# Attention heads issued in pairs, and a state-space scan folded by four steps

## The chip, the cores and the metric

The kernel runs on one core of one Trainium2 chip. Its time is the device time of that core in microseconds (us), taken as the median of several executions. A profile of one execution gives each engine's instructions: PE is TensorE (matmuls), PEld its weight loads, DVE VectorE, ACT ScalarE, POOL GpSimd, SP the engine that issues most DMAs.

## The reference, cut to what matters

The program is two transformer-like blocks of two layers over 256 tokens of width 1024. Three attentions and one scan are touched by the change:

```
swa:   s = q k^T * scale, masked to |i-j| <= 128; p = softmax with a sink logit; o = p v   (8 heads on 2 key heads)
diff:  s_c = q_c k_c^T * scale (c = 0, 1); a = softmax(s_0) - lam * softmax(s_1); o = a v  (4 heads)
stick: z = q k^T * scale; w = exp(log_sigmoid(z) + sum of log_sigmoid(-z) over later keys); o = w v  (16 heads)
S5:    x_t = lb * x_(t-1) + bb u_t  (complex, 32 groups of 64 states),  y_t = Re(c x_t) + d u_t
```

The first block has both layers of swa and diff (the mixer); the second block has an S5 layer with a pooling branch, then a stick-breaking layer, each followed by a mixture of 16 experts (MoE).

## The kernel before

All weights stream from memory through a ring of 1 MB tiles. `Ring.pump` issues the next load on SP's queue as soon as a slot is free; the order of loads is fixed. Large matmuls split each f32 operand in a high and a low part and add three products (`S` L381, `T` L390, `proj_T` L435); small ones are plain f32, and each such call shows as two MATMUL instructions. `bank("w")` and `bank("acc")` are two sets of four PSUM banks. The order of the work is written out by hand: every engine runs its instructions in the order in which the program emits them.

**Mixer** (L899). Each step projects one weight unit (some 5.6 us of PE), rotates it, and weaves in one piece of each attention. `swa_scores` (L822) makes the scores of two heads that lie on partitions 0 to 63 and 64 to 127: for each head and each half of the queries one 64-row matmul (L830), then a bf16 mask product over all 128 rows (L833). `diff_scores` (L866, matmul L873) makes first both halves for c = 0, then both for c = 1, again 64 rows each, and without a mask. `swa_soft` and `diff_soft` follow on DVE and ACT.

**S5.** `s5_params` (L1170) makes the tables while the feed-forward layer before runs: it is a generator whose 18 pieces are emitted at the ends of the iterations 2 to 19 of that layer (`hooks`, L2368). The recurrence is folded by two steps, so a scan has 128 columns. POOL builds tables of cosines and sines of 128 columns by doubling (L1232 to L1251); DVE, PE and ACT build the input matrices `BT` (transposes, L1269), the output matrices `CT` and one matrix `K0` (L1304). `s5_layer` (L1345) then has eight rounds of two state blocks each. `inputs(i)` (L1405) is 8 calls over 32 rows with 128 columns; `turned_in(i)` multiplies by the tables (two DVE products, L1414 and L1415, and two POOL sums); `scan(i)` has four scans of 128 columns (L1428), two more products and two POOL sums into `S`. `outputs(h)` (L1435) multiplies `S` by `CT` (L1445, 32 output columns, four next to one another in the array) after `K0` (L1440), once for each half of the state blocks. Between the rounds PE makes the pooling branch (`vproj`, `pooled`, `poolproj`). When `outputs(1)` is emitted, `scanned()` gives the memory of the tables and of `S` to the ring, for the expert weights. Then `trow` (L399) begins the output product.

**Stick-breaking** (`sb_layer`, L2119). `scores` of one head: 64 rows, 256 and 128 columns (L2156, L2157), Abs, Exp, Ln on ACT (L2159 to L2161), one DVE and one POOL operation. `weights`: two bf16 mask products (L2170, L2171), three plain products (L2172 to L2174), Exp on ACT (L2176). `av`: two products into 64 output columns (L2183, L2184). `advance` runs scores of head h, weights of head h-2 and av of head h-4; two steps stand after each of the query and key projections, and the last eight close the stage.

```
            if h < 16:
                step1(h)
            if 2 <= h < 18:
                step2(h - 2)
            if 4 <= h < 20:
                step3(h - 4)
```

Of the kernel before, what the change touches and what calls it, by code (L numbers as in the profile page):

```python
# [8 lines left out]
F32 = mybir.dt.float32  # L9
# [73 lines left out]
class K:  # L83
# [738 lines left out]
    def swa_scores(self, b):  # L822

        nc = self.nc
        outs = []
        for kv in range(2):
            rows = slice(64 * kv, 64 * kv + 64)
            sv = self.bank("acc").rearrange("p (q k) -> p q k", q=2)
            for qt in range(2):
                nc.tensor.matmul(sv[:, qt, :], self.sq[rows, b, qt * P:qt * P + P], self.sk[rows, 0, :],  # L830
                                 start=True, stop=False)
                kb, mk = ((1, self.maskA), (0, self.maskB))[qt]
                nc.tensor.matmul(sv[:, qt, kb * P:kb * P + P], self.ident16, mk, start=False, stop=True)  # L833
            outs.append(sv)
        return outs
# [30 lines left out]
    def diff_scores(self, h):  # L866
        nc = self.nc
        outs = []
        for c in range(2):
            rows = slice(64 * c, 64 * c + 64)  # L870
            sv = self.bank("acc").rearrange("p (q k) -> p q k", q=2)
            for qt in range(2):
                nc.tensor.matmul(sv[:, qt, :], self.dq[rows, h, qt * P:qt * P + P], self.dk[rows, h, :],  # L873
                                 start=True, stop=True)
            outs.append(sv)
        return outs
# [267 lines left out]
    def s5_alloc(self, pool):  # L1144
        t = lambda shape, name: pool.tile(shape, F32, name=name)
        self.tc_, self.ts_ = t([P, 16, P], "s5c"), t([P, 16, P], "s5s")
        self.BT = [[t([P, 4, P], f"BT{c}{b}") for b in range(2)] for c in range(2)]
        self.CT = [t([P, 16, 32], f"CT{i}") for i in range(4)]
        self.K0 = t([P, 4, P], "K0")
        self.prm = t([P, 7, 16], "s5prm")  # L1150
        self.dcol, self.pscale = (self.cp.tile([P, 4], F32, name=n) for n in ("s5d", "pscale"))

# [17 lines left out]
    def s5_params(self, tp):  # L1170
# [7 lines left out]
        for t in BD + [self.K0]:  # L1178
            G.memset(t, 0.0)
# [20 lines left out]
        lbr, lbi, fr, fi, m2, c2, s2 = (self.prm[:, i] for i in range(7))  # L1200
        V.tensor_mul(lbr, mag, cs)
        V.tensor_mul(lbi, mag, sn)
        V.tensor_mul(m2, mag, mag)
        V.tensor_mul(t1, sn, sn)
        V.tensor_scalar(c2, t1, -2.0, 1.0, op0=ALU.mult, op1=ALU.add)
        V.scalar_tensor_tensor(s2, sn, 2.0, cs, op0=ALU.mult, op1=ALU.mult)
# [18 lines left out]
        wc, ws, w2 = sm("wc", [P, 16]), sm("ws", [P, 16]), sm("w2", [P, 16])  # L1225
        G.tensor_copy(wc, c2)
        G.tensor_copy(ws, s2)
        G.memset(self.tc_[:, :, 0:1], 1.0)
        G.memset(self.ts_[:, :, 0:1], 0.0)
        tm = sm("tm", [P, 16, 32])  # L1230
        k = 1
        while k < P:  # L1232
# [13 lines left out]
            if k < P:  # L1246
# [31 lines left out]
        bb = [sm(f"bb{c}", [P, 16, 16]) for c in range(2)]  # L1278
        halves = [(slice(0, 64), lambda t: t[:, :, 0:16]), (slice(64, P), lambda t: t[:, :, 16:32])]
        cmul(bb[0], bb[1], bc16(fr), bc16(fi), b_re, b_im, u, v)  # L1280
        yield
        for c in range(2):
            for rows, o in halves:
                V.tensor_copy(o(BD[c])[rows], bb[c][rows])
        yield
        flat = lambda t: t.rearrange("p n h -> p (n h)")
        for c in range(2):
            transposed(self.BT[c][1].rearrange("p q s -> p (q s)"), flat(BD[c]))
        yield
# [6 lines left out]
        for c, cd in enumerate(cds):  # L1296
            transposed(flat(self.CT[c]), cd.rearrange("p q g s -> p (q g s)"), -1.0 if c else None)
        yield

        pt = self.bank()[:, :P].rearrange("p (q o) -> p q o", q=4)  # L1300
        for n in range(16):
            q, r = divmod(n, 4)
            for c in range(2):
                nc.tensor.matmul(pt[32 * r:32 * r + 32, q, :], BD[c][:, n], self.CT[c][:, n],  # L1304
                                 start=(c == 0), stop=(c == 1))
        yield
        for r in range(4):
            rows = slice(32 * r, 32 * r + 32)
            V.tensor_copy(self.K0[rows, :, rows], pt[rows])
        yield  # L1310
        cmul(BD[0], BD[1], bc16(lbr), bc16(lbi), bb[0], bb[1], u, v, halves)
        yield
        for c in range(2):
            transposed(self.BT[c][0].rearrange("p q s -> p (q s)"), flat(BD[c]))
        yield
        bc32 = lambda a: a[:, :, None].to_broadcast([P, 16, 32])
        u, v = (tp.tile([P, 16, 32], F32, tag="cd", name=n_, bufs=2) for n_ in ("u2", "v2"))
        cr, nci, c1r, nc1i = self.CT
        V.tensor_mul(u, cr, bc32(lbr))
        V.tensor_mul(v, nci, bc32(lbi))  # L1320
        V.tensor_add(c1r, u, v)
        yield
        V.tensor_mul(u, nci, bc32(lbr))
        V.tensor_mul(v, cr, bc32(lbi))
        V.tensor_sub(nc1i, u, v)
# [19 lines left out]
    def s5_layer(self, wk, sc, projected, row, head, scanned):  # L1345
# [4 lines left out]
        uT = wk.tile([P, 4, 2, P], F32, tag="uT", name="uT")  # L1350
        pT = wk.tile([P, 4, 256], F32, tag="vT", name="pT")
        yT = wk.tile([P, 4, 256], F32, name="yT")
# [6 lines left out]
        S = [sc.tile([P, 2, 2, P + 1], F32, name=f"S{i}") for i in range(4)]  # L1359
# [14 lines left out]
        def u_tr(c, tt):  # L1374
# [4 lines left out]
            for m in range(2):  # L1379
                V.tensor_copy(uT[:, 2 * c + m, :, 64 * tt:64 * tt + 64],  # L1380
                              b[:, m * P:m * P + P].rearrange("p (j b) -> p b j", b=2))
# [11 lines left out]
        lbr, lbi, fr, fi, m2, c2, s2 = (self.prm[:, i] for i in range(7))  # L1393
        xb, st, ybank, pbank = {}, {}, {}, {}
        pair = lambda i: (8 * (i // 4) + i % 4, 8 * (i // 4) + i % 4 + 4)
        rows_of = lambda n: slice(32 * (n % 4), 32 * (n % 4) + 32)

        def inputs(i):

            x = xb[i] = self.bank().rearrange("p (n c j) -> p n c j", n=2, c=2)  # L1400
            for m, n in enumerate(pair(i)):
                rows = rows_of(n)
                for c in range(2):
                    for b in range(2):
                        mm(x[:, m, c], self.BT[c][b][rows, n // 4], uT[rows, n // 4, b],  # L1405
                           start=(b == 0), stop=(b == 1))

        def turn(src, i):

            n = pair(i)[0]  # L1410
            bc = lambda t: t[:, n:n + 5:4, None, :].to_broadcast([P, 2, 2, P])
            p = self.sp.tile([P, 2, 2, P], F32, tag="rt", name="s5p", bufs=3)
            q = sc.tile([P, 2, 2, P], F32, tag="s5q", name="s5q", bufs=2)
# [4 lines left out]
        def turned_in(i):  # L1418
            p, q = turn(xb.pop(i), i)
            v = st[i] = self.sp.tile([P, 2, 2, P], F32, tag="qs", name="s5v", bufs=3)  # L1420
            G.tensor_add(v[:, :, 0], p[:, :, 0], q[:, :, 1])
            G.tensor_sub(v[:, :, 1], p[:, :, 1], q[:, :, 0])

        def scan(i):
            z = st.pop(i)
            for m, n in enumerate(pair(i)):
                for c in range(2):
                    V.tensor_tensor_scan(z[:, m, c], m2[:, n:n + 1].to_broadcast([P, P]), z[:, m, c], 0.0,  # L1428
                                         op0=ALU.mult, op1=ALU.add)
            p, q = turn(z, i)  # L1430
            s = S[i % 4]
            G.tensor_sub(s[:, :, 0, 1:], p[:, :, 0], q[:, :, 1])
            G.tensor_add(s[:, :, 1, 1:], p[:, :, 1], q[:, :, 0])

        def outputs(h):  # L1435

            bank = self.bank().rearrange("p (q b j) -> p q b j", q=2, b=2)
            for q in (2 * h, 2 * h + 1):
                y = bank[:, q % 2]
                mm(y[:, 0], self.K0[:, q], uT[:, q, 0], start=True, stop=False)  # L1440
                for t, (b, c) in enumerate(((0, 0), (0, 1), (1, 0), (1, 1))):
                    for r in range(4):
                        n = 4 * q + r
                        s = S[r][:, q % 2, c]
                        mm(y[rows_of(n), b], self.CT[(2, 3, 0, 1)[t]][:, n], s[:, b:b + P],  # L1445
                           start=(b == 1 and c == 0), stop=(c == 1))
# [29 lines left out]
        ph = wk.tile([P, 4, 256], F32R, name="ph")  # L1476
        pl = wk.tile([P, 4, 256], F32R, name="pl")
# [42 lines left out]
        inputs(0)  # L1520
        inputs(1)
        turned_in(0)
        inputs(2)
        for i, (c, tt) in enumerate(((0, 0), (0, 1), (1, 0))):
            vproj(c, tt)
            turned_in(i + 1)
            scan(i)
            inputs(i + 3)
            if i == 1:
                projected()  # L1530
        inputs(6)
        turned_in(4)
        nc.scalar.preload_act_table_set("sigmoid_and_others")
        scan(3)
        outputs(0)
        inputs(7)
        turned_in(5)
        scan(4)
        vproj(1, 1)
        yhl = self.xp.tile([P, 2, 4, 256], F32R, tag="xl", name="gyhl")  # L1540
        yh, yl = yhl[:, 0], yhl[:, 1]
        turned_in(6)
        scan(5)
        for g in range(4):
            pooled(g)
        turned_in(7)
        scan(6)
        for g in range(4):
            poolproj(g)
        scan(7)  # L1550
        for g in range(4):
            poolrest(g)
        head.load(self.sp, "rt", 3)
# [27 lines left out]
        ol = wk.tile([P, 4, 256], F32R, tag="vT", name="gol")  # L1581
        for mp in range(2):
# [13 lines left out]
            for m in range(2):  # L1596
                il = lambda t: t[:, 2 * mp + m].rearrange("p (j b) -> p b j", b=2)
# [889 lines left out]
```

## Time and profile before

| what | value |
|---|---|
| median of 3 runs | 1816.9 us (1815.74 to 1817.62) |
| the profiled execution's own time | 1816.69 us |
| its span, first to last instruction | 1814.9 us |
| PE busy | 1734.9 us (96%) |
| DVE, ACT, POOL busy | 939.3, 713.9, 379.4 us |
| mean granted TensorE clock | 0.983 |
| DMA | 421.41 MB, mean 232 GB/s |

The span leaves out some 1.8 us around it. Busy time says where an engine has work, not where it is at its peak; a window table gives it for a stretch, with the granted clock (1.00 is 2.4 GHz, 0.50 is 1.2 GHz) and the DMA share. In the timeline rows the columns are start, duration, engine, line, operation, output and inputs, shape and count; a bracket gives the engine's idle time before it and what ended that.

### The profile page before, as it was taken

Reading aid. Unit: us, or ns where it says so; the run is one execution under the profiler, and the core shown is the slowest. Engines: PE = TensorE matmul, PEld = TensorE weight load, DVE = VectorE, ACT = ScalarE, POOL = GpSimd, SP = SyncE. Lnnn points to the kernel's source line nnn. Section 1 sums busy time; section 2 is a strip of 40 time slices with the busy share of each in tenths; the row PEclk is TensorE's granted clock in tenths of the full one; section 3 lists DMA queues with packets and bytes.
Section 4 is the critical chain, followed back from the end, with each engine's and each line's share of the span. In section 5 each row is a group of like instructions: output and inputs, shape, how many; then the busy total and the mean of one; then the engine's idle time right before and its main releaser. Section 6 shows DMA issues by size and latency. Waiting matters only on the chain. (4 is left out here: it accounts for less than half of the span.)

```text
span 1814.9 us, 27041 instructions
## 1 busy us (share of the span) xinstructions
PE 1734.9 (96%) x11023; PEld 1351.0 (74%) x11023; DVE 939.3 (52%) x1513; ACT 713.9 (39%) x1252; POOL 379.4 (21%) x435
## 2 busy tenths in 40 slices
PE   9999999999999999998999998899998999899996
PEld 8999877899989998877999886445454987445542
DVE  5655677654565545767677797422223524422223
ACT  5444446444444444564454425312112555212111
POOL 1000454100020002636084364200001213100001
PEclk9999999999999999999999989999999999999998
DMA  9655533565555655526454546699997837599994
GB/s 293 222 189 178 179 100 98 170 213 178 178 190 182 198 180 157 140 71 195 162 190 163 164 164 270 254 414 414 410 419 257 279 100 282 215 414 414 412 419 162
DMA packets 189481, 421.41 MB, mean 232 GB/s; under 512 B 7264, under 2 KB 142736, under 8 KB 165280
## 3 DMA queue, kind: packets, MB, share of 16 engines
q1 hardware_dynamic: 184848, 405.82, 61.9%
q0 software_dynamic: 3920, 12.95, 2.4%
q8 instruction: 91, 1.49, 0.3%
q10 hardware_dynamic: 576, 0.77, 0.1%
q14 instruction: 46, 0.38, 0.1%
HBM read 418.47 MB, written 1.05 MB: 231 GB/s over the span
## 5 line engine op out<-in xcount | busy, mean ns | idle before, releaser
L386 PE MATMUL bank_w<-xh,unit 128*128 128x256 f32 x1504 | 425.7, 283 | 0.0
L388 PE MATMUL bank_w<-xh,unit 128*128 128x256 f32 x1504 | 422.6, 281 | 0.1
L387 PE MATMUL bank_w<-xl,unit 128*128 128x256 f32 x1504 | 422.2, 281 | 0.0
L337 DVE TENSOR_TENSOR unit<-ring,unit 128x1024 fp32r<-128x1024 f32 (+2 forms) x220 | 275.8, 1290 | 49.6 <-ACT unit L336 45.4
L386 PEld LDWEIGHTS bank_w<-xh,unit 128*128 128x128 f32 x1504 | 283.2, 188 | 3.8 <-ACT za L2161 0.5
L387 PEld LDWEIGHTS bank_w<-xl,unit 128*128 128x128 f32 x1504 | 283.4, 188 | 3.1 <-issue 0.5
L388 PEld LDWEIGHTS bank_w<-xh,unit 128*128 128x128 f32 x1504 | 283.3, 188 | 0.3 <-DVE unit L337 0.3
L336 ACT CAST unit<-ring 128x1024 fp32r<-128x1024 f32 (+2 forms) x297 | 248.2, 891 | 5.5 <-DMA ring<-in_ffn_w_in_dram 5.4
L337 POOL TENSOR_TENSOR unit<-ring,unit 128x512 fp32r<-128x512 f32 (+1 forms) x77 | 113.4, 1490 | 606.0 <-ACT unit L336 606.0
L1897 PE MATMUL bank_w<-ring,xg 128*64 128x512 f32 x1024 | 223.2, 593 | 0.0
L378 DVE TENSOR_TENSOR rl<-ring,rh 128x1024 fp32r<-128x1024 f32 x104 | 130.2, 1253 | 171.6 <-ACT rh L373 171.3
L1897 PEld LDWEIGHTS bank_w<-ring,xg 128*64 128x64 f32 x1024 | 74.1, 137 | 139.8 <-issue 139.0
L373 ACT CAST rh<-ring 128x1024 fp32r<-128x1024 f32 x108 | 113.1, 1049 | 115.8 <-PE bank_acc L401 115.8
L399 PE MATMUL bank_acc<-rh,gg 128*128 128x512 f32 x352 | 139.3, 396 | 0.0
L401 PE MATMUL bank_acc<-rh,gg 128*128 128x512 f32 x352 | 138.6, 394 | 0.0
L400 PE MATMUL bank_acc<-rl,gg 128*128 128x512 f32 x352 | 138.4, 393 | 0.0
L1947 PE MATMUL bank_w<-ring,hT 128*64 128x512 f32 x512 | 113.4, 595 | 2.1 <-issue 2.1
L259 POOL TENSOR_SCALAR s_ld<-s_m,s_mu 128x1 f32<-128x1 f32 x20 | 16.6, 828 | 436.7 <-DVE s_mu L250 436.7
L1911 DVE CAST ohT<-bank_w 128x256 fp32r<-128x256 f32 x16 | 6.8, 424 | 191.9 <-PE bank_w L1907 191.9
L574 ACT ACTIVATE sg<-bank_w 128x256 f32<-128x256 f32 x76 | 29.2, 384 | 182.5 <-PE bank_w L388 179.8
L1947 PEld LDWEIGHTS bank_w<-ring,hT 128*64 128x64 f32 x512 | 37.9, 137 | 68.3 <-issue 66.8
L401 PEld LDWEIGHTS bank_acc<-rh,gg 128*128 128x128 f32 x352 | 66.0, 188 | 14.6
(502 smaller groups left out, 2639.2 us busy)
## 6 DMA issues: line engine op xcount, KB each, us to landing
ring<-in_moe_w_dram SPq DMA_DIRECT2D x188, 1024.0 KB, 13.9
ring<-in_ffn_w_in_dram SPq DMA_DIRECT2D x86, 1024.0 KB, 5.5
ring<-in_ffn_w_out_dram SPq DMA_DIRECT2D x44, 1024.0 KB, 5.2
ring<-in_w_in_dram SPq DMA_DIRECT2D x18, 1024.0 KB, 6.2
ring<-in_sb_w_qkv_dram SPq DMA_DIRECT2D x12, 1024.0 KB, 11.7
ring<-in_ple_w_gate_dram SPq DMA_DIRECT2D x8, 1024.0 KB, 18.0
ring<-in_w_out_dram SPq DMA_DIRECT2D x8, 512.0 KB, 5.8
ring<-in_w_out_dram SPq DMA_DIRECT2D x4, 1024.0 KB, 5.6
```

The lines of the kernel that those rows point to most:

```text
L336: copy = lambda sel=sel, src=src: self.nc.scalar.copy(sel(hi), src)
L337: sub = lambda eng=eng, sel=sel, src=src: eng.tensor_sub(sel(lo), src, f(sel(hi)))
L373: (copy or self.nc.scalar.copy)(hi, src)
L378: (lo_eng or self.nc.vector).tensor_sub(lo, src, f(hi))
L386: self.nc.tensor.matmul(out, a, self.xh[:, k, :], start=(k == 0), stop=False)
L387: self.nc.tensor.matmul(out, a, self.xl[:, k, :], start=False, stop=False)
L388: self.nc.tensor.matmul(out, b, self.xh[:, k, :], start=False, stop=(k == 7))
L399: mm(acc[tt][h], a, hi[:, cols], start=first, stop=False)
L400: mm(acc[tt][h], a, lo[:, cols], start=False, stop=False)
L401: mm(acc[tt][h], b, hi[:, cols], start=False, stop=last)
L1897: nc.tensor.matmul(b[64 * e:64 * e + 64], xg[:, 4 * kh + k, c0 + 64 * e:c0 + 64 * e + 64], ws[e][0][:, 512 * k:512 * k + 512], start=(kh = ...
L1947: nc.tensor.matmul(yb[h][64 * e:64 * e + 64], hT[:, jj, 64 * e:64 * e + 64], w, start=(jj == 0), stop=(jj == 3))
```

## The change

Mixer: `swa_scores` and `diff_scores` take two banks first and issue the two heads' 64-row products next to one another, and swa's two masks after both. Stick-breaking: a step of `advance` is a pair of heads, with scores of pair p, weights of pair p-1 and av of pair p-2; the products of the two heads alternate. S5: the recurrence is folded by four steps (64 columns); the tables have 64 columns, with a decay table `mt_` so that one scan runs over four blocks; there are four `BT`, four `CT` pairs and three `KT`; the scratch of the tables lies in `CT[3][0]`. All input products stand in one block ahead of the rounds; there are four rounds of four blocks; both `outputs` follow the last scan. Four 4 KB tiles for `BT` (pool `s5b`) are used again for `yT`, `pT`, `ph`, `pl`.

```
 def swa_scores(self, b):
+        outs = [self.bank("acc").rearrange("p (q k) -> p q k", q=2) for _ in range(2)]
+        for qt in range(2):
+            for kv, sv in enumerate(outs):
+                rows = slice(64 * kv, 64 * kv + 64)
                 nc.tensor.matmul(sv[:, qt, :], self.sq[rows, b, qt * P:qt * P + P], self.sk[rows, 0, :],
                                  start=True, stop=False)
+            kb, mk = ((1, self.maskA), (0, self.maskB))[qt]
+            for sv in outs:
                 nc.tensor.matmul(sv[:, qt, kb * P:kb * P + P], self.ident16, mk, start=False, stop=True)
...
 def s5_params(self, tp):
+        for r in range(4):
+            V.tensor_copy(self.mt_[:, r, :, 1:], t1[:, r::4, None].to_broadcast([P, 4, 63]))
...
-        while k < P:
+        while k < 64:
...
+        def spread(k):
+            b, nb = bb[k % 2], bb[(k + 1) % 2]
             for c in range(2):
+                for rows, o in halves:
+                    V.tensor_copy(o(BD[c])[rows], b[c][rows])
+            if k < 3:
+                cmul(*nb, bc16(lbr), bc16(lbi), *b, u, v)
...
+        for k in range(4):
+            for c in range(2):
+                transposed(self.BT[c][3 - k].rearrange("p q s -> p (q s)"), flat(BD[c]))
+            if k < 3:
+                pt = self.bank()[:, :P].rearrange("p (q o) -> p q o", q=4)
+                for n in range(16):
+                    q, r = divmod(n, 4)
+                    for c in range(2):
+                        nc.tensor.matmul(pt[32 * r:32 * r + 32, q, :], BD[c][:, n], self.CT[0][c][:, n],
+                                         start=(c == 0), stop=(c == 1))
+                spread(k + 1)
+                for r in range(4):
+                    rows = slice(32 * r, 32 * r + 32)
+                    V.tensor_copy(self.KT[k][rows, :, rows], pt[rows])
+            yield
...
+        for k in range(3):
+            (cr, nci), (c1r, nc1i) = self.CT[k], self.CT[k + 1]
+            V.tensor_mul(u, cr, bc32(lbr))
...
 def s5_layer(...):
+        def inputs():
+            for r in range(4):
+                xb[r] = self.bank().rearrange("p (c q j) -> p c q j", q=4, c=2)
+            for q in range(4):
                 for c in range(2):
+                    for b in range(4):
+                        for r in range(4):
+                            mm(xb[r][:, c, q], self.BT[c][b][rows_of(r), q], uT[rows_of(r), q, b],
+                               start=(b == 0), stop=(b == 3))
...
+        def scan(r):
+            z = st.pop(r)
+            for c in range(2):
+                flat = z[:, c].rearrange("p q j -> p (q j)")
+                V.tensor_tensor_scan(flat, self.mt_[:, r].rearrange("p q j -> p (q j)"), flat, 0.0,
+                                     op0=ALU.mult, op1=ALU.add)
...
 def outputs(h):
+                for k in range(3):
+                    mm(y[:, k:3], self.KT[k][:, q], uT[:, q, 0:3 - k], start=(k == 0), stop=False)
+                for b in range(4):
+                    for c in range(2):
+                        for r in range(4):
+                            n = 4 * q + r
+                            s = S[r][:, c, q, b // 3:b // 3 + 64]
+                            mm(y[rows_of(r), b], self.CT[(b + 1) % 4][c][:, n], s,
+                               start=(b == 3 and c == 0), stop=(b >= 2 and c == 1))
...
+        inputs()
         turned_in(0)
+        vproj(0, 0)
+        turned_in(1)
+        scan(0)
+        vproj(0, 1)
+        turned_in(2)
+        scan(1)
+        vproj(1, 0)
         nc.scalar.preload_act_table_set("sigmoid_and_others")
+        turned_in(3)
+        scan(2)
+        vproj(1, 1)
+        projected()
         scan(3)
...
         for g in range(4):
             poolrest(g)
+        outputs(0)
         head.load(self.sp, "rt", 3)
         rowsplit(0, V)
         outputs(1)
...
 def advance(n):
+                p = done[0]
                 done[0] += 1
+                if p < 8:
+                    zs[p] = scores(*qks[p])
+                if 1 <= p < 9:
+                    ws[p - 1] = [weights(*zp) for zp in zs.pop(p - 1)]
+                if 2 <= p < 10:
+                    step3(p - 2)
...
         for c in range(4):
             nk = self.plain_unit()
             q = qk(unit, 0.125)
             if c:
-                advance(2)
+                advance(1)
```

## Rows read from the trace of the kernel before

**Rows 1.** The page: the span.

```profile
span 1814.9 us, 27041 instructions
```

**Rows 2.** Window table: stretch, length, busy time of each engine (instructions), clock, DMA share, GB/s.

```profile
262.51:276.97 14.46, 14.46 (x95) 10.48 (x94) 12.17 (x25) 7.61 (x26) 5.88 (x4) 0.96 0.14 42
...
900.00:1000.00 100.00, 100.00 (x779) 93.89 (x779) 75.31 (x115) 46.41 (x66) 61.42 (x82) 1.00 0.56 187
...
1051.38:1101.20 49.82, 44.32 (x385) 38.85 (x384) 48.32 (x76) 12.61 (x24) 31.82 (x37) 0.84 0.31 109
...
1495.04:1516.31 21.27, 21.27 (x129) 16.05 (x128) 8.76 (x14) 14.46 (x31) 5.08 (x7) 1.00 0.35 117
...
1200.00:1250.00 50.00, 49.65 (x241) 24.27 (x240) 10.99 (x21) 7.51 (x12) 0.00 (x0) 1.00 1.02 411
```

**Rows 3.** Timeline of PE in the mixer: swa's scores, then diff's.

```profile
260.15 0.70 PE L830 MATMUL bank_acc<-sk,sq 64*128 64x256 f32 x2
260.78 0.23 PE L833 MATMUL bank_acc<-hconsts 128*128 128x128 bf16 x1
260.94 0.70 PE L830 MATMUL bank_acc<-sk,sq 64*128 64x256 f32 x2
...
262.51 1.14 PE L873 MATMUL bank_acc<-dk,dq 64*128 64x256 f32 x8
```

**Rows 4.** Waits of DVE in the mixer, 240 to 292 us: total, times, longest.

```profile
DVE s_su L892 <- ACT prob L889: 4.3, 3, 1.5
DVE s_nm L843 <- PE bank_acc L833: 2.1, 3, 0.9
```

**Rows 5.** Timeline of the S5 layer: input products, one round, the end.

```profile
1051.38 6.88 PE L1405 MATMUL bank_w<-uT,BT 32*128 32x128 f32 x48
...
1057.82 2.58 DVE L1428 TENSOR_TENSOR_SCAN s5v<-s5prm,s5v 128x128 f32<-128x128 f32 x4
...
1061.64 0.68 DVE L1414 TENSOR_TENSOR s5p<-bank_w,s5c 128x512 f32<-128x512 f32 x1
...
1062.41 1.86 PEld L1405 LDWEIGHTS bank_w<-uT,BT 32*128 32x128 f32 x16
...
1066.68 0.68 DVE L1414 TENSOR_TENSOR s5p<-bank_w,s5c 128x512 f32<-128x512 f32 x1
...
1096.50 2.18 PE L1445 MATMUL bank_w<-S,CT 128*32 128x128 f32 x26 [3.20 <-POOL S L1432]
...
1099.34 1.94 PE L1445 MATMUL bank_w<-S,CT 128*32 128x128 f32 x32
...
1101.20 0.78 PE L399 MATMUL bank_acc<-rh,ph 128*128 128x512 f32 x1
```

**Rows 6.** Window table in the S5 layer, where the granted clock was at half.

```profile
1054.04:1060.87 6.83, 6.83 (x36) 6.61 (x35) 6.80 (x10) 0.00 (x0) 3.94 (x5) 0.50 0.85 307
...
1095.00:1101.83 6.83, 5.30 (x62) 3.59 (x63) 5.19 (x9) 2.05 (x5) 6.09 (x4) 0.50 0.13 41
```

**Rows 7.** Timeline of PE: transposes and products of the table pieces.

```profile
940.30 1.04 PE L1269 MATMUL bank_w<-consts,BD 128*128 128x128 f32 x8
...
967.47 0.86 PE L1304 MATMUL bank_w<-CT,BD 128*32 128x32 f32 x64
```

**Rows 8.** Timeline of stick-breaking: heads 0 and 1 together, then one head's step.

```profile
1444.26 0.71 PE L2156 MATMUL bank_acc<-qk 64*128 64x256 f32 x4
...
1503.40 0.70 PE L2156 MATMUL bank_acc<-qk 64*128 64x256 f32 x2
...
1504.26 0.23 PE L2170 MATMUL bank_acc<-hconsts 128*128 128x128 bf16 x1
...
1504.36 0.49 ACT L2159 ACTIVATE za<-bank_acc 128x384 f32<-128x384 f32 x1 [0.81 <-PE bank_acc L2157]
...
1505.40 0.65 PE L2183 MATMUL bank_w<-zw,sbv 128*64 128x256 f32 x2
...
1505.87 0.47 ACT L2176 ACTIVATE zw<-bank_acc 128x384 f32<-128x384 f32 x1
...
1506.19 0.70 PE L2156 MATMUL bank_acc<-qk 64*128 64x256 f32 x2
```

More of the change, by code (lines that the diff above doesn't have):

```diff
@@ L867, in diff_scores @@
         nc = self.nc
[L868 to L872, printed above, removed]
+        outs = [self.bank("acc").rearrange("p (q k) -> p q k", q=2) for _ in range(2)]
+        for qt in range(2):
+            for c, sv in enumerate(outs):
+                rows = slice(64 * c, 64 * c + 64)
                 nc.tensor.matmul(sv[:, qt, :], self.dq[rows, h, qt * P:qt * P + P], self.dk[rows, h, :],
                                  start=True, stop=True)
-            outs.append(sv)
         return outs
@@ L1358, in s5_layer @@
             G.dma_start(t.rearrange("p g c -> p (g c)"), self.consts[:, NC0 + 512 + 768 * i:NC0 + 1280 + 768 * i])
-        S = [sc.tile([P, 2, 2, P + 1], F32, name=f"S{i}") for i in range(4)]
+        S = [sc.tile([P, 2, 4, 65], F32, name=f"S{i}") for i in range(4)]
         for s in S:
@@ L1392, in s5_layer, with turn @@
         vu.append(self.plain_unit((G, V)))
-        lbr, lbi, fr, fi, m2, c2, s2 = (self.prm[:, i] for i in range(7))
         xb, st, ybank, pbank = {}, {}, {}, {}
[L1395 to L1402, printed above, removed]
-                for c in range(2):
[L1404 to L1413, printed above, removed]
+        rows_of = lambda r: slice(32 * r, 32 * r + 32)
+        def inputs():
+            for r in range(4):
+                xb[r] = self.bank().rearrange("p (c q j) -> p c q j", q=4, c=2)
+            for q in range(4):
+                for c in range(2):
+                    for b in range(4):
+                        for r in range(4):
+                            mm(xb[r][:, c, q], self.BT[c][b][rows_of(r), q], uT[rows_of(r), q, b],
+                               start=(b == 0), stop=(b == 3))
+        def turn(src, r):
+            bc = lambda t: t[:, None, r::4, :].to_broadcast([P, 2, 4, 64])
+            p = self.sp.tile([P, 2, 4, 64], F32, tag="rt", name="s5p", bufs=3)
+            q = sc.tile([P, 2, 4, 64], F32, tag="s5q", name="s5q", bufs=2)
             V.tensor_mul(p, src, bc(self.tc_))
@@ L1416, in turn, with turned_in @@
             return p, q
[L1418 to L1433, printed above, removed]
+        def turned_in(r):
+            p, q = turn(xb.pop(r), r)
+            v = st[r] = self.sp.tile([P, 2, 4, 64], F32, tag="qs", name="s5v", bufs=3)
+            G.tensor_add(v[:, 0], p[:, 0], q[:, 1])
+            G.tensor_sub(v[:, 1], p[:, 1], q[:, 0])
@@ L1474, in out_gelu @@
             yield
-        ph = wk.tile([P, 4, 256], F32R, name="ph")
-        pl = wk.tile([P, 4, 256], F32R, name="pl")
+        yT, pT = (self.s5_b(i, [P, 4, 256], n) for i, n in ((0, "yT"), (3, "pT")))
+        ph, pl = (self.s5_b(i, [P, 4, 256], n, F32R) for i, n in ((1, "ph"), (2, "pl")))
         def vproj(c, tt):
@@ L2193, in step2, with av @@
-        def step2(h):
-            ws[h] = weights(*zs.pop(h))
-        ob = {}
-        def step3(h):
-            p = h // 2
-            if h % 2 == 0:
-                ob[p] = self.bank()[:, :256]
-            av(ob[p], ws.pop(h), h)
-            if h % 2 == 1:
-                o = ob.pop(p)
-                nc.scalar.copy(yh[:, p, :], o)
-                V.tensor_sub(yl[:, p, :], o, f(yh[:, p, :]))
-        qks = {}
-        ready = []
-        done = [0]
+        def av(o, ws, p):
+            parts = [(o[64 * e:64 * e + 64], w, slice(P * p + 64 * e, P * p + 64 * e + 64)) for e, w in enumerate(ws)]
+            for oe, w, cols in parts:
+                mm(oe[:, :], v[:, 0, cols], w[:, 0:256], start=True, stop=False)
+            for oe, w, cols in parts:
+                mm(oe[:, P:256], v[:, 1, cols], w[:, 256:384], start=False, stop=True)
@@ L2233, in sb_layer @@
             if c:
-                advance(2)
+                advance(1)
         projected()
```

211 lines of the change are left out of this document (77 added, 134 removed).

## The prediction

> **What bounds the kernel now.** I read the page first: PE has work 96% of the span [rows 1], so the question for every part is whether PE waits there. The window table answers it by stage [rows 2]. In the mixer and in the last eight heads of stick-breaking PE is busy for the whole window. In the feed-forward layer that hosts the table pieces it is full too, while DVE has work 75 us of 100 and POOL 61. The S5 stage differs: DVE has 48.32 of 49.82 us, PE 44.32 at a mean clock of 0.84, so DVE sets the pace. In the MoE layer PE is at 49.65 of 50 although the DMA engines are saturated (1.02). Its loads start when `outputs(1)` gives memory back, before and after the change, so what S5 gains shifts that layer whole. Then I read single instructions: the timelines of the mixer, the S5 stage, the table pieces and stick-breaking [rows 3, 5, 7, 8], and DVE's waits in the mixer [rows 4].
>
> The profiled execution took 1816.69 us, 0.2 below the median. The sum is made against 1816.7. A measurement of this kernel can tell some 0.2% from no change, 3.6 us.
>
> **Mixer.** `diff_scores` is reordered, not reduced. Its eight matmuls take 1.14 us now [rows 3], while two of swa's, which stand alone between masks, take 0.70: if nothing overlapped eight would take about 2.6. So the two row groups already run beside one another and the reorder is worth nothing (bounds 0 and 1.4 us a call, eight calls; the row takes the lower). `swa_scores` does change: a mask of all 128 rows stands between the two heads. From one pair of products to the next is 260.94 - 260.15 = 0.79 us, so a call with four takes 3.15. Afterwards a half takes about 0.63 for four matmuls in two row groups plus two masks of 0.08 to 0.23 [rows 3], 0.85 together; a call takes 1.7 and PE saves 1.45, eight times: 11.6 us. Not all of it arrives. DVE has 12.17 of the 14.46 us of such a step [rows 2] and in 52 us lost 4.3 to ACT but only 2.1 to swa's scores [rows 4]. What PE gives up beyond that turns into PE waiting for DVE. Three us a layer is what the wait row and its neighbours allow; I take **-6** (bounds 0 and -11.6).
>
> **Table pieces, in the second feed-forward layer.** PE gets 16 more transposes (eight take 1.04 us: 2.0) and 128 more products for the two additional `K` matrices (64 take 0.86: 1.7) [rows 7], and some 0.6 for turning between tile shapes: +4.3. DVE gets some 46 more small operations, about 19 us: the block spreads, the copies of `KT`, three `CT` products a step. POOL loses the last doubling, some 20 us. DVE has a quarter of the stage free [rows 2], which hides 19 us over seven iterations if they fall evenly. By my count an iteration that hosts a `K` piece has 10.4 us of DVE work against 10.1 of PE, so a little shows. I take **+4.5** (bounds +3.7 and +8). If the cover were gone, see the slower rival.
>
> **S5.** Now a round takes 1066.68 - 1061.64 = 5.04 us, eight times, with four scans in about 2.6 [rows 5]. Afterwards there are four rounds with the same four DVE products of 128x512, 0.6 to 0.68 each, 2.42, and two scans of 256 columns in place of four of 128. The trace has no such scan. If its price goes by columns, two cost 2.4 (I take this: the columns are the same in number); if by instruction, 1.3. A round is 4.85, four are 19.4 against 40.3.
>
> For that the inputs come in one block first: 256 matmuls of 64 columns over 32 rows. Each has a weight load; 16 loads took 1.86 us [rows 5], 0.116 each, 64 for each of four row groups. If the groups overlap wholly that is 7.4 us; at the pace of the present block, 48 in 6.88 or 0.143 for each matmul of a group, 9.2; if only two groups overlap, 14.3; if none, 28.7. I take 9.2, as the row is the same kind of block, partly with the clock at half (1054.04 to 1060.87 [rows 6]). It starts some 0.6 later, since it needs all four banks, and ends at 1061.2. Four rounds end at 1080.6, POOL's last sums at 1081.5.
>
> Both `outputs` now stand behind the last scan, uncovered; today half of them lies under the rounds. They are 256 products of 64 columns on `CT` and 24 full-array ones on `KT`. Thirty-two of 128 columns took 1.94 us at the end [rows 5], when the granted clock was at half [rows 6]. By columns 256 of 64 take 7.8 at that clock and 3.9 at full. `KT` adds 3 to 6, less one group that can run ahead of the wait. So the bounds are 7 and 13; I take 9.5, since the clock came back after 6.8 us both times in the rows. The output product then starts at 1091.0 where it started at 1101.2: **-10.2** (bounds -5 and -15). SP's queue is not moved against this: `scanned()`, which lets the ring load again, still stands at `outputs(1)`, so the loads come earlier by the same 10 us. The four small `s5b` tiles wait only for products long done.
>
> **Stick-breaking.** One head's step now is 1506.19 - 1503.40 = 2.79 us [rows 8]: scores 0.86, weights 1.14, av 0.79; a pair 5.58. Heads 0 and 1 stand together, as no weights are due yet, and their four score products take 0.71, as long as the two of a single head: two row groups are free in pairs. `av` writes 64 columns, and alternating heads lets two column groups run together: two now take 0.65 [rows 8]; I take 0.81 for four. Weights stay at 2.1 to 2.3. A pair is then 0.87 + 2.1 + 0.1 + 0.81 = 3.9, so 1.7 less. Pair 0 saves nothing, pair 1 0.9, pairs 2 to 4 1.7 each, as these stand among projections that bound PE: 6.0. In the tail there is no projection to hide ACT. Its work for a head is from 1504.36 to 1506.34, 2.0 us [rows 8], so 4.0 a pair, against 3.9 of PE; and with four `acc` banks the scores of pair p+1 wait for the Exp of pair p-1, which ACT has behind the six activations of pair p. I put a tail pair at 4.95, so the 21.27 us [rows 2] become 18.0: -3.2. Together **-9.2** (bounds -6 and -12).
>
> **Sum:** 1816.7 - 6 + 4.5 - 10.2 - 9.2 = 1795.8, **1796 us**, 1.1% less. By the terms' own bounds it lies between 1782 and 1814; errors in them are separate, and my band for this case is 1788 to 1802.
>
> **Rivals.**
> *A, PE's savings arrive whole:* DVE's waits on ACT in the mixer move up with PE, and the outputs run at full clock. For it: PE is gapless in both attention stages. Against: DVE's 84% in a mixer step, and ACT in the tail. -11 + 4 - 14.5 - 11: about 1784.
> *B, the small products don't pack:* the input block with two groups at a time or half the clock (+5), outputs cold (+3), ACT in the tail holds more, swa gives 4. For it: the clock was at half in the present block and again at the end [rows 6], and a short stage with waits is where this happens. -5 + 7 - 8 - 4: about 1807.
> *C, the other side:* DVE becomes the bound of the host layer. A `K` piece rewrites the block scratch that PE's products of the same piece still read, and DVE is in order: the split of the next projection's operand stands behind that wait, and PE behind the split. For it: three such pieces and three `CT` ones, DVE at 75% before anything is added. Against: PE reaches those products some us before DVE needs the scratch, and the splits are about 1.6 us ahead. It decides where a split is not ready by more than that. Then the pieces' DVE time falls on PE, 3 x 5.6 + 3 x 4.1 = 29 us in place of 4.5, which is more than the -25.4 of the rest: about 1820, 0.2% slower; with B's losses (-17 in place of -25.4) 1829.
> *D, the change does more than I count:* consecutive matmuls of the same row group hold each other up, so that only neighbours on different groups overlap. Then the eight `diff_scores` products, issued group after group, hold PE for something between the 1.14 us of the row and 2.6, and alternating them halves that: 0.6 to 1.3 a call, I take 0.7, 5.6 us in all: about 1790. The row of eight in 1.14 us [rows 3] speaks against it, since serially they would need 2.6. The Trainium skill has this as a rule ("TensorE: Matmul & The Clock Gate", Part 3, The mechanism): matmuls start and end strictly in program order. By it the diff reorder would be a gain in its own right; the trace contradicts that, as eight products in program order by group took less than half their serial time.
>
> **How the numbers follow.** Forecast case 0.60, A 0.17, B 0.15, C 0.05, D 0.03. The range has to reach into A and B: 1783 to 1809, leaving out C, half of A's lower half and part of B's upper end. Slower by over 0.2% needs C with B's losses: 0.03. Within 0.2%: 0.03, C alone or B at its worst. Faster: 0.94.
>
> **What would show it.** In the changed kernel's profile: from the first input product to the output product's first matmul some 39.6 us (now 49.8), of which an input block of about 9 and four rounds of 4.85; scans of 256 columns near 1.2 us; the outputs line after a POOL wait, 9 to 10 long, with the clock at half for part of it. In the mixer four score matmuls and two masks in 0.85 and DVE's wait on swa's scores gone, with PE now waiting for DVE or ACT. In the feed-forward layer PE still full between table pieces, and the layer about 4.5 longer; PE waiting on DVE there would be rival C. In the tail of stick-breaking pairs about 4.95 apart, PE waiting on ACT's release of `acc` banks. An input block of 14 us or more, or a tail that stays at 21 us, would make the prediction wrong upwards; diff products below 1 us a call downwards.

## The result and the profile after

The changed kernel takes 1793.29 us (median of 4 runs, 1792.64 to 1794.33); the one before 1816.55 beside it. The ratio is 0.9872, 95% interval 0.9855 to 0.9889: 1.3% faster. The forecast was 1796 and a range of 1783 to 1809.

The page and the window table of the changed kernel: a stretch in the mixer, the S5 stage, its half-clock part, the tail of stick-breaking (columns as in [rows 2]).

```profile
span 1791.5 us, 27789 instructions
...
258.00:274.38 16.38, 14.52 (x107) 10.25 (x107) 14.06 (x27) 7.79 (x26) 6.85 (x5) 1.00 0.20 65
1052.56:1090.52 37.96, 33.63 (x658) 31.66 (x657) 27.48 (x36) 12.91 (x24) 24.52 (x21) 0.96 0.41 145
1083.28:1086.70 3.42, 3.42 (x71) 3.13 (x71) 1.27 (x3) 0.00 (x0) 3.42 (x1) 0.50 0.32 81
...
1479.20:1495.18 15.98, 14.83 (x99) 10.29 (x100) 7.49 (x13) 13.03 (x29) 5.08 (x7) 1.00 0.42 148
```

PE is no longer full in the mixer (14.52 of 16.38) nor in the tail (14.83 of 15.98; the last line stops 1.4 us before the tail's end): part of what it gave up came back as waiting. Lining up the same PE instruction in both profiled traces gives a ledger of how far the changed kernel is ahead:

| stage | forecast | measured |
|---|---|---|
| two mixers | -6 | -6.1 |
| table pieces | +4.5 | +5.8 (4.3 up to the last piece's products, 1.5 at the layer's end, 1.3 of it one wait) |
| S5 | -10.2 | -11.9 |
| stick-breaking | -9.2 | -10.2 |
| last layer norm | 0 | -2.6 |
| clock at half elsewhere, and rest | 0 | +1.6 |
| span | -20.9 | -23.4 |

**Mixer.** PE's timeline in the changed kernel; it answers to [rows 3]:

```profile
270.59 0.66 PE L817 MATMUL bank_w<-consts,prob 128*128 128x128 f32 x4 [1.50 <-ACT dv L936]
271.18 0.70 PE L829 MATMUL bank_acc<-sk,sq 64*128 64x256 f32 x4
271.81 0.28 PE L833 MATMUL bank_acc<-hconsts 128*128 128x128 bf16 x2
272.03 0.70 PE L829 MATMUL bank_acc<-sk,sq 64*128 64x256 f32 x4
...
272.88 1.14 PE L871 MATMUL bank_acc<-dk,dq 64*128 64x256 f32 x8
```

A half costs 0.85 us as forecast (272.03 - 271.18), diff's eight still 1.14. Each of the eight calls is 1.45 shorter, 5.8 in a mixer. More than half of that came back as waits, 3.3 us in the first mixer. The longest is in the bracket: PE waits for a PSUM bank in which ACT's copy of `dv` is still due.

**S5.** The timeline of the stage, PE and DVE; it answers to [rows 5]:

```profile
1052.56 0.44 PE L1417 MATMUL bank_w<-uT,BT 32*128 32x64 f32 x6
1053.30 6.21 PE L1417 MATMUL bank_w<-uT,BT 32*128 32x64 f32 x210 [0.30 <-DVE uT L1393]
1060.31 1.34 PE L1417 MATMUL bank_w<-uT,BT 32*128 32x64 f32 x40 [0.80 <-issue]
...
1062.77 0.68 DVE L1425 TENSOR_TENSOR s5p<-bank_w,s5c 128x512 f32<-128x512 f32 x1
1063.96 2.03 DVE L1440 TENSOR_TENSOR_SCAN s5v<-s5m,s5v 128x256 f32<-128x256 f32 x2
1066.02 1.04 DVE L1425 TENSOR_TENSOR s5p<-s5v,s5c 128x512 f32<-128x512 f32 x1
1067.59 0.68 DVE L1425 TENSOR_TENSOR s5p<-bank_w,s5c 128x512 f32<-128x512 f32 x1
...
1077.23 0.88 PE L1453 MATMUL bank_w<-uT,K 128*128 128x192 f32 x6
1081.51 0.32 PE L1459 MATMUL bank_w<-S,CT 128*32 128x64 f32 x8 [2.73 <-POOL S L1444]
1083.09 1.60 PE L1453 MATMUL bank_w<-uT,K 128*128 128x192 f32 x6
...
1090.52 0.50 PE L399 MATMUL bank_acc<-rh,ph 128*128 128x512 f32 x1
```

The block takes 9.1 us, a round 1067.59 - 1062.77 = 4.82, the outputs after POOL's `S` 9.0: forecast 9.2, 4.85 and 9.5. The stage is 37.96 long in place of 49.82. The clock was at half for 3.4 us of it here and for 17.1 us before.

**Stick-breaking.** PE's timeline of the tail; it answers to [rows 8]:

```profile
1479.20 0.70 PE L2163 MATMUL bank_acc<-qk 64*128 64x256 f32 x4
1482.23 0.65 PE L2192 MATMUL bank_w<-zw,sbv 128*64 128x256 f32 x4
1483.67 0.86 PE L2163 MATMUL bank_acc<-qk 64*128 64x256 f32 x3 [0.57 <-ACT zw L2185]
1488.32 0.86 PE L2163 MATMUL bank_acc<-qk 64*128 64x256 f32 x3 [0.38 <-ACT zw L2185]
...
1496.56 0.50 PE L399 MATMUL bank_acc<-rh,sbyh 128*128 128x512 f32 x1
```

Four products in the time of two, for scores and for `av`; tail pairs are 4.5 to 4.65 apart (forecast 4.95), with the wait on ACT's Exp that was named. The tail is 1496.56 - 1479.20 = 17.36 us long in place of 21.27. One more thing changed here than the section on the change lists: `weights` makes one product on `negtri` over 384 columns in place of two over 256 and 128. A pair's weights take 2.17 us (1480.06 to 1482.23) in place of 2.30, so this is a small part of the gain; no run has it alone.

### The profile page after: what moved, and what is told of

Read it like the earlier page. It is cut to its first block, busy times and chain, and to the rows that moved or that the text cites. A ratio compares the mean times of both kernels' runs of the same rounds, so it can differ in the third digit from the quotient of the medians.

```text
span 1791.5 us, 27789 instructions
## 1 busy us (share of the span) xinstructions
PE 1704.7 (95%) x11407; PEld 1328.9 (74%) x11407; DVE 929.0 (52%) x1523; ACT 712.7 (40%) x1256; POOL 348.2 (19%) x403
## 5 line engine op out<-in xcount | busy, mean ns | idle before, releaser
L337 DVE TENSOR_TENSOR unit<-ring,unit 128x1024 fp32r<-128x1024 f32 (+2 forms) x220 | 270.4, 1266 | 51.4 <-ACT unit L336 47.3
L337 POOL TENSOR_TENSOR unit<-ring,unit 128x512 fp32r<-128x512 f32 (+1 forms) x77 | 113.3, 1488 | 628.9 <-ACT unit L336 628.9
L1960 ACT CAST yhl<-bank_w 128x512 fp32r<-128x512 f32 x32 | 18.7, 586 | 147.3 <-PE bank_w L1952 147.3
```

Of the source, the lines that this page charges most:

```text
L337: sub = lambda eng=eng, sel=sel, src=src: eng.tensor_sub(sel(lo), src, f(sel(hi)))
```

## The experiments

**e1, e2, e3: the parts alone.** Each is the kernel before with one third of the diff: the two score functions; the stick-breaking functions; the S5 functions.

> The kernel before with only the two score functions of the mixer reordered. In the changed kernel every one of the eight swa_scores calls is 1.45 us shorter on TensorE, 11.6 us in all, but the two mixers end only 6.1 us earlier, since TensorE then waits for PSUM banks that ACT and DVE empty late. Theory: the parts are independent, so this kernel is 6 us faster than before (about 1810.5), with the same waits in the mixer. Rival (the rest of the 6 us came from the clock, which was at half for 3.4 us in each mixer of before): 3 to 4 us faster only where the clock still falls there. Second rival, the gain needs the other parts: 0.

> The kernel before with only stick-breaking in pairs. Theory: a pair costs 1.77 us less among the projections and 0.9 less in the tail, the stage 10.2 us less, as in the changed kernel: about 1806.4. If ACT's six activations of a pair set the tail whatever the scores do: 7 us less, 1809.5. The last stage (from the last combining product to the end) took 15.4 us before and 12.8 after the change; if that belongs to stick-breaking (its tiles, its queue) it is 12.8 here too and the gain 12.8; if it comes from where DVE's code lies, it may fall out either way, as this kernel has nearly as many DVE instructions as before.

> The kernel before with only the folded scan and its tables. Theory: +4.3 us of TensorE work in the feed-forward layer, +1.3 for one DVE wait at its end, -11.9 in the S5 stage: 6 to 6.5 us faster, about 1810.3. It has the DVE instructions of the changed kernel up to the end of S5, so if the 2.6 us of the last stage come from where DVE's code lies, they are gone here too: then 9 us faster, about 1807.7. Rival: the scan's gain in the changed kernel was the clock's (17 us of the S5 stage at half before, 3.4 after), and comes out otherwise here: 0 to 4 us.

Medians against the kernel before on the same chip (1818.07): 1812.86 (ratio 0.9971, interval 0.9962 to 0.9981), 1809.51 (0.9951, 0.9934 to 0.9968), 1810.11 (0.9949, 0.9932 to 0.9965), that is -5.2, -8.6 and -8.0, together -21.8 where the whole change gave -23.3: within the scatter, as independent parts would. The traces show the stages of the changed kernel again: mixers -3.0 each in e1, stick-breaking -10.2 in e2, table pieces +5.8 in e3. S5 differs: -10.0 in e3, whose clock was at half for 13.7 us from the input block on, against -11.9. The single spans scatter by more than the stages do: e1's profiled execution was only 1.2 us below the old one. It lost 2.2 us between the mixers, 1.5 ahead of S5 and 1.1 behind it, each time with 3.4 us or more at half clock that the old one did not have. The last stage was short (2.6 us less) in e3 alone; e3's median is 1810.1 all the same, not the 1807.7 forecast for that case.

e1 can't tell how much of the mixer's 3 us is the clock's, since its clock was at full in both mixers and the old one's was at half for 3.4 us in each. e3 can: it has the old order, and its two mixers differ in the clock. The lines give a mixer from its first score product to the first transposes of diff's output (columns as in [rows 2]): the first of the kernel before, both of e3, the first of the changed kernel, the first of e12.

```profile
236.97:307.01 70.04, 68.80 (x436) 52.81 (x436) 52.59 (x110) 39.99 (x116) 29.62 (x24) 0.98 0.29 87
...
236.79:305.93 69.14, 67.55 (x436) 51.85 (x436) 52.34 (x110) 39.69 (x116) 29.62 (x24) 1.00 0.30 88
748.11:818.17 70.06, 68.80 (x437) 52.80 (x436) 52.61 (x110) 39.97 (x116) 29.65 (x24) 0.98 0.28 87
...
238.51:305.48 66.97, 62.46 (x436) 48.84 (x436) 51.95 (x110) 39.02 (x116) 29.59 (x24) 1.00 0.30 90
...
236.88:303.86 66.98, 63.81 (x436) 49.54 (x435) 51.95 (x110) 39.02 (x116) 29.58 (x24) 0.97 0.30 91
```

In the old order a mixer takes 69.1 us at full clock (one mixer) and 70.0 with a stretch at half; in the new order 67.0 either way. So the reorder gains 2.2 us a mixer at equal clock, and 0.9 came with the clock. The stretch at half stands in seven of the eight mixers with the old order and, e10 aside, in one of eighteen with the new. That the reorder keeps the clock up is likely by this count, but how is not shown.

**e4: diff in its old order**, all else changed.

```
-        for qt in range(2):
-            for c, sv in enumerate(outs):
+        for c, sv in enumerate(outs):
+            for qt in range(2):
```

> The changed kernel with diff_scores in its old order (both halves of the queries for c = 0, then both for c = 1). Theory: eight products take 1.14 us in either order, so 0 (1793.3, within 0.1%). Rival, in which consecutive products on the same rows hold each other up: 0.6 to 1.3 us a call, 5 to 10 us slower.

1794.88 us, ratio 0.9875 (0.9857 to 0.9893) where the changed kernel has 0.9872. PE's timeline of this kernel:

```profile
259.53 1.14 PE L872 MATMUL bank_acc<-dk,dq 64*128 64x256 f32 x8
```

The same 1.14 as in the new order: rival D falls.

**e5: 16 more DVE instructions** in the kernel before, at its start.

```
+            for _ in range(16):
+                self.nc.vector.memset(pad, 0.0)
```

> The kernel before with 16 memsets of one column added to DVE at the start of the program, where it has nothing to do. Theory: DVE's jump over the code that is not taken, ahead of the last layer norm, took 3.15 us before (from the branch to the next instruction) and 0.55 after the change, because its target lay in code that had yet to be loaded; ten more DVE instructions ahead of it moved that target. So with 16 more the jump takes about 0.55 and the kernel is 2.6 us faster (about 1814), at no less work. Rival: the 3.15 us are a wait for TensorE or the clock: 0.

DVE's first instruction of the last layer norm in the kernel before, in the changed one and here:

```profile
1801.56 0.69 DVE L246 SCALAR_TENSOR_TENSOR lnr<-ple,bank_acc 128x512 f32<-128x512 f32 x1 [3.06 <-DVEq L2043]
```

```profile
1778.10 0.69 DVE L246 SCALAR_TENSOR_TENSOR lnr<-ple,bank_acc 128x512 f32<-128x512 f32 x1 [0.45 <-DVEq L2048]
```

```profile
1800.68 0.69 DVE L249 SCALAR_TENSOR_TENSOR lnr<-ple,bank_acc 128x512 f32<-128x512 f32 x1 [0.45 <-DVEq L2046]
```

The bracket names DVE's own sequencer at a jump. With no work removed the wait falls from 3.06 to 0.45. The median, 1815.56 (0.9991, 0.9981 to 1.0001), shows 1.6 of the 2.6 us and alone would not settle it; the row does. So 2.6 us of the result belong to where DVE's code lies, not to anything that the change does.

**e6: input products by row group.**

```
-            for q in range(4):
-                for c in range(2):
-                    for b in range(4):
-                        for r in range(4):
+            for r in range(4):
+                for q in range(4):
+                    for c in range(2):
+                        for b in range(4):
```

> The changed kernel with the 256 input products of S5 ordered by row group (64 products on rows 0 to 31, then on 32 to 63, and so on) in place of taking turns. Theory: four row groups run beside one another only when products on different groups stand next to one another; each group's 64 products take some 7.5 us, so the block grows from 9.1 to about 30 us, DVE can begin after the first group, and the output product comes about 6 us later. Rival: products of 64 columns are bounded by their issue, 9 us in any order, and DVE then begins 7 us earlier: 5 us faster.

1829.89 us in a single run, 36.6 above the changed kernel. PE's timeline and two windows of the block:

```profile
1051.62 49.28 PE L1417 MATMUL bank_w<-uT,BT 32*128 32x64 f32 x256
```

```profile
1051.62:1055.20 3.58, 3.58 (x33) 3.58 (x33) 3.37 (x4) 1.65 (x4) 3.48 (x3) 1.00 1.00 361
1055.20:1100.00 44.80, 44.80 (x223) 44.80 (x223) 10.91 (x15) 0.00 (x0) 8.29 (x10) 0.50 0.11 39
```

Without turns nothing overlaps: 0.11 us a product at full clock (33 in 3.58 us) and 0.20 at half (223 in 44.80), and the clock stays at half though PE never rests. At full clock 256 in a row would take about 28 us by the first figure (an estimate), near the 30 that I had said; the rest of the 49.3 is the clock's. In turns the block takes 9.1 us, and 12.6 with most of it at half clock (e3, e8).

**e7: the KT products first.**

```
+        direct(0)
+        direct(1)
         outputs(0)
```

> The changed kernel with the 24 products on KT of all four column groups ahead of the ones on S (in the changed kernel only the first six are). TensorE waits 2.73 and 0.37 us for POOL's S there, and the other 18 take 3.65 us behind the wait. Theory: the uncovered outputs shrink from 9.0 to about 6 us, the kernel is 2.5 to 3 us faster (1790.5), and up to 1.4 more if TensorE, busy in that wait, keeps its full clock. Rival: S is later than it seems and the wait just moves: 0.

`direct` holds the KT products of both halves. Each column group started its PSUM bank here, which drops part of the KT sum; the instructions are the same. 1792.61 (0.9858, 0.9842 to 0.9875), single runs at 1789.5, 1790.1, 1795.1 and 1797.2: above the 1790.5 forecast, and not clear of the changed kernel's 0.9872. The profiled one was the slowest: half clock from 1057.6 to 1071.3, a block of 12.6 us, and PE late for the KT products.

**e8: two pieces in one iteration.**

```
             transposed(flat(self.CT[0][c]), cd.rearrange("p q g s -> p (q g s)"), -1.0 if c else None)
-        yield
         def spread(k):
```

> The changed kernel with two pieces of the table generator emitted in one iteration (the transposes of C, which are TensorE's and ACT's, and the first spread, which is DVE's), so that the generator ends an iteration earlier. Theory: the last piece's six CT products (4.1 us of DVE) no longer stand ahead of the last gate product of the feed-forward layer, and the 1.27 us that TensorE waited for it are gone: 1.2 us faster (1792.1). Rival: the wait reappears at another iteration: 0.

1795.90 (0.988, 0.9864 to 0.9897): no gain. The wait at the end went, as expected (-1.3), but DVE and PE at the merged piece show:

```profile
939.55 1.40 DVE L1271 TENSOR_TENSOR u<-s5prm,bb 128x256 f32<-128x256 f32 x1
...
943.25 3.42 DVE L337 TENSOR_TENSOR unit<-ring,unit 128x1024 fp32r<-128x1024 f32 x2
...
947.05 0.39 PE L386 MATMUL bank_w<-xh,unit 128*128 128x256 f32 x1 [3.06 <-DVE sg L575]
```

The merged spread now runs while POOL builds its tables. The same DVE operation takes 0.42 us in the changed kernel, after POOL is done, and 1.40 here. The split behind it (L337) is held back and PE waits for what follows. That is rival C in small: one piece too much and PE waits 3.06.

**e9 and e10: the changed kernel again, and three edits**: KT first with each bank started once, the generator's second and third piece together (light ones, so all later pieces move one iteration forward), and `dvproj` ahead of the next unit's split.

```
-        v1 = self.plain_unit(GV)
         dvproj(0, v0)
+        v1 = self.plain_unit(GV)
...
         R, Q, L = (rql[:, i] for i in range(3))
-        yield
```

> The changed kernel once more, on the chip of the next run, as its measure. Theory: 0.9872 of the kernel before, with single executions some 5 us apart, since the clock is at half for 3.4 us of the S5 stage in one and for 13.7 in another (seen in the experiments before this one). Rival: those lengths belonged to the edits there; then all executions of this kernel lie within 2 us.

> The changed kernel with three edits: the KT products of all four column groups ahead of the ones on S, each PSUM bank started once; the table generator's second and third piece in one iteration, which moves all later pieces one iteration forward; and dvproj emitted ahead of the next unit's split in the mixer. Theory: the 18 KT products fill TensorE's wait of 3.1 us (-2.5), the wait of 1.27 at the end of the feed-forward layer goes and does not come back, since no iteration gets a heavier piece than it had neighbours for (-1.3), and ACT empties dvproj's bank before it splits the next unit, so the waits of 1.5 and 0.3 us in each mixer go (-2 to -3.5 in all, if nothing else is late there): 5.5 to 7 us faster than the changed kernel. Rivals: the mixer's units come late instead (0 from the third edit), 3.8 faster; the KT products stand behind a TensorE that is itself late when the clock is at half in the input block (0.8 in place of 2.5).

e9: 1795.59 (0.9889, 0.9872 to 0.9906), executions from 1793.05 to 1800.37: the scatter is the changed kernel's own. e10: 1791.91 (0.9864, 0.9849 to 0.9879). That is 3.7 us less than e9, the rivals' 3.8 and not the 5.5 to 7 forecast, with intervals that overlap. The wait at the layer's end went; one of 0.5 us (PE for DVE's split) stands ahead of it now, and the layer's pieces cost 4.3 in place of 5.8. The third edit gave nothing: the first wait shrank, but the clock was at half for 6.8 us in each mixer afterwards, and both were 0.4 to 0.6 longer. With the block at half clock again, KT first brought 0.8 behind the block against e8, whose block had the same clock: the rival's figure.

**e11 and e12: the wait at the layer norm filled** with two unread matmuls; e12 also has the first two of e10's edits.

```
+                for i in range(2):
+                    nc.tensor.matmul(b, self.ident, x[:, 0, 0:512], start=(i == 0), stop=(i == 1))
                 turn(x, 1)
```

> The changed kernel with two matmuls of 128x512 whose result nobody reads, put where TensorE waits 2.35 us for a layer norm (six places, one of them 9 us ahead of S5's input block). In five traces the clock was at half at that wait and again for 6.8 to 13.7 us from the input block on; in three it was at full there, and the block then took 9.1 us in place of 12. Theory: that the clock falls in the block follows from TensorE's standing still at the layer norm, so with the wait filled the block takes 9.1 us, the half-clock stretch at the wait is gone in every execution, and the median is that of the fast executions or below (1792 to 1793.5), with all within 2 us of one another. Rival: the block itself, small products on 32 rows, brings the clock down by chance: executions of 1793 and 1798 to 1800 as before.

> The same filled waits, with the KT products ahead and the second and third piece in one iteration (the first two of the three edits before). Theory: -1.3 at the end of the feed-forward layer and -2.5 to -3 at the outputs, now that TensorE is early enough to do the KT products in its wait: 1788.5. Rival: TensorE's stream of 256 products stops for 1.3 to 1.8 us on its own issue whatever stands ahead (1.34 and 1.82 in the two traces with KT first): 1790.

e11: 1794.10 (0.987, 0.9854 to 0.9887), 1792.87 to 1796.50. The half-clock stretches at the waits are gone from its trace, yet the clock was at half from 1053.7 to 1067.4 and the block took its long form:

```profile
1051.88 12.21 PE L1423 MATMUL bank_w<-uT,BT 32*128 32x64 f32 x250 [0.30 <-DVE uT L1399]
```

So my theory fell: standing still at the layer norm is not what the block's clock needs to fall. The traces of the kernel before, of e5 and of e6 had said so already: in each the clock was at full at that wait and then at half for 6.8, 10.2 and 51.2 us from the block on. e12: 1791.77 (0.9855, 0.9838 to 0.9871), lowest 1788.54. In its trace PE stops for its own issue in the block and in the outputs:

```profile
1059.15 3.69 PE L1422 MATMUL bank_w<-uT,BT 32*128 32x64 f32 x63 [1.37 <-issue]
...
1079.96 3.19 PE L1471 MATMUL bank_w<-uT,K 128*128 128x192 f32 x24
...
1086.92 1.40 PE L1462 MATMUL bank_w<-S,CT 128*32 128x64 f32 x82 [1.16 <-issue]
```

It beats the kernel before surely. Its ratio is below the changed kernel's 0.9872 with intervals that overlap, and below e9's 0.9889 with intervals that just miss one another. It is 3.3 us above the 1788.5 forecast and 1.8 above the rival's 1790. The stop of 1.16 is the rival's; 1.34 and 1.82 in the other two traces with KT first (e10, e7).

## Why the prediction was right

- *Mixer, -6:* -6.1, right in part by luck. At equal clock the reorder gains 2.2 us a mixer, 4.3 in all; the other 1.8 came as the clock stayed at full, and the sum had no term for that. More than half of the 11.6 came back as waiting, as forecast, but the step "what PE gives up beyond that turns into PE waiting for DVE" named the lesser of two engines. PE's waits in the first mixer, before and after:

```profile
PE bank_w L1010 <- DVE pT L114: 0.7, 1, 0.7
...
PE bank_w L817 <- ACT dv L936: 1.8, 2, 1.5
PE bank_w L1007 <- DVE pT L114: 0.7, 1, 0.7
PE bank_w L860 <- DVE pT L114: 0.7, 1, 0.7
PE bank_w L443 <- DVE rt L807: 0.4, 1, 0.4
PE bank_w L1007 <- ACT pT L112: 0.4, 1, 0.4
```

  Of 3.3 us of new waits 2.2 are for ACT and 1.1 for DVE. The largest is ACT's copy, behind four casts of a unit on its queue; without banks to write in, PE stands. Diff's order is worth nothing, as the row of eight said (e4). The 2.6 us that the prediction took for eight without overlap is too much: a lone pair's 0.70 holds a start that a row pays once, and other plain f32 products of 256 columns follow one another 0.215 us apart (two of L1503 from 1072.89 to 1073.32), so about 2.0 (an estimate); 1.14 is well below that too. The Trainium skill's rule, matmuls that start and end in program order ("TensorE: Matmul & The Clock Gate", Part 3, The mechanism), would have had the reorder gain; e4 shows no gain for these eight, while e6 shows a full loss of overlap for 64 products in a row on one group. What brings the eight together in the old order is not shown.
- *Table pieces, +4.5:* the iterations with K products and transposes are 4.3 us longer in sum, the figure of PE's terms; the other pieces cost nothing under DVE's cover. The rest is the layer's end, 1.5 with one wait of 1.3, in the bounds, and e10 removed that wait.
- *S5, -10.2:* measured -11.9, and -10.0 in e3 with the input block at half clock, so the size depends on which clock an execution meets. The block's 9.2 was right for a wrong reason. Its 0.143 a product came from three rounds of the old kernel that stand on one row group each, partly at half clock. The new block's pace was 0.118 a product of a group (210 in 6.21, four groups), the lower bound's, and two stops, 0.30 and 0.80 us idle and 1.6 from start to start, made up the rest. In the round two errors cancelled: two scans took 2.03, between the ends (I took 2.4), and the first product after them 1.04 in place of 0.68, beside a POOL sum. The other 1.7 us are the 0.6 by which the block did not start later, 0.2 of the block, 0.4 of the four rounds and 0.5 of the outputs (9.0 for 9.5).
- *Stick-breaking, -9.2:* -10.2; pairs 1.77 less (1.7 forecast), the tail 3.9 less (3.2), as ACT held it up less. Four `av` products took 0.65, as long as two, where I had 0.81.
- *What the sum lacked:* -2.6 at DVE's jump (e5), and +1.6 of clock. Without the jump the result would stand near the forecast; with it the sum is 2.5 short. The nearness of single stages owes something to luck with the clock: 1.8 us in the mixers, and 1.9 in S5 by e3. Rivals A, B and C did not occur as a whole; e3, e7, e8, e10 and e11 show B's half-clock block in single executions. B's own sum took S5 at -5, which leaves out its 3 us of cold outputs; with them it is about 1809.5.

What stays open: why the clock falls in the input block in one execution (13.7 us) and not in another, and why it stays up in the mixer in the new order.

## What to carry to other kernels

Issue products on different row or column groups next to one another when something else stands between them, and check in the timeline whether they overlap already. Before counting PE's gain, list who empties its PSUM banks, on ACT as on DVE: more than half of the mixer's gain stopped there. Compare stages, not only totals, below 0.3%, and stages at the same clock: one jump's place and the clock moved whole runs by as much as a part of this change.

## What the runs showed that was not expected

- DVE lost 3.06 us at a jump over code that is not run, 0.45 with 16 instructions more ahead of it. The Trainium skill says that a taken branch whose target is not in the instructions already fetched must wait for them ("Runtime: NRT & Kernel Launch", Instruction fetch mechanics); the rows agree. In the trace of the kernel before, three loads of instructions start between 1798.6 and 1799.9 us and the last ends at 1801.2, just ahead of DVE's next instruction at 1801.4; in the changed kernel DVE goes on 0.55 us after its branch.
- PE, in streams of products of 64 columns, stopped 0.42 to 1.82 us on its own issue in six traces (0.42 in e4, 0.61 in e9, 0.80 in the changed kernel, 1.16 to 1.82 in e7, e10 and e12), once or twice in a stage. Why is not shown.
- A product of 64 columns on 32 rows takes as long as one of 128, 0.11 us at full clock on one row group (33 in 3.58 us in e6; 16 in 1.86 [rows 5]).
- A scan of 256 columns took 1.0 us where one of 128 took 0.65 [rows 5]: the price is neither by instruction nor by column.
- A DVE product of two operands in SBUF took 0.42 us with POOL at rest and 1.40 beside POOL's table products (e8).
